# Three of sixteen output-projection blocks in other product forms, and four weight splits on GpSimd

## The chip, the cores and the metric

The kernel runs on one core of one Trainium2 chip. The metric is the device time of one execution in microseconds (us), as the median of the runs shown. TensorE (PE) multiplies, and its weight loads (PEld) are recorded apart from its matmuls. VectorE (DVE), ScalarE (ACT) and GpSimd (POOL) work elementwise, and SyncE (SP) issues most of the DMA transfers.

## What is computed

One layer of a streaming encoder runs for 256 frames of a new stream and 64 frames of a running one, 320 positions in all; all matrices are 32-bit floats. What the change touches is the output projection behind the merge of two branches, and its residual add:

```
def layer(x, l, cache_k, cache_v, norm_mix, w_in, b_gate, ..., w_out, norm_ffn, w_gate_up, w_down):
    ...
    merged = g_a * (a @ w_branch_a[l]) + g_b * (bb @ w_branch_b[l])
    h = x + merged @ w_out[l]
    hn = rmsnorm(h, norm_ffn[l])
    gu = hn @ w_gate_up[l]
    ...
```

`merged` is 320 x 2048 and `w_out` is 2048 x 2048.

## The kernel before, in words

Features lie on partitions and the 320 positions (`T`) in the free dimension. A weight matrix is cut into blocks of 128 output features; the host lays each block out as 128 x (chunks x 128). `block` (L87) multiplies one block with all its chunks of 128 input features and sums the products in one PSUM tile `acc` of which three exist. The blocks follow one another in the order of the program: the input projection, its two branches, `w_out`, then the feed-forward weights. The output projection is the loop `for m in range(KD)` at L659 to L666, sixteen blocks of sixteen chunks.

A 32-bit product is made of three matmuls in the rounded 32-bit type `F32R`. Every activation is kept as a high and a low part, and every weight tile is split in the same way while it streams in. `weights` (L68) fetches eight chunks (a half-block, 128 x 1024, 512 KB) on SP's queue into `raw`, of which there are three buffers. ACT casts it to `wh` (L75) and DVE subtracts to get `wl` (L76); there are four buffers of each. `product` (L80) then issues, for one chunk, `wh` times the high part (L83), `wh` times the low part (L84) and `wl` times the high part (L85), each 320 columns wide. In the output projection the high and low parts are named `mh` and `ml`. So a half-block has 24 matmuls and a block 48.

Some small matmuls elsewhere take plain 32-bit operands (`F32`) and are not split: the diagonal attention scores (L416), part of the attention output (L488), the gating mix (L602, L604), and the sums at the end (L721, L723). The trace prints the type of both kinds as f32, so the line tells which it is; a plain 32-bit matmul of the program stands in the trace as two matmul records, each with its own weight load (L604 is called 16 times and has 32 records).

After each block of the output projection, DVE adds the residual `xr` (L664), ACT and DVE split the result times a gain for the feed-forward part (`gained`, L121), ACT squares it (L197) and GpSimd adds the square to a running sum (L198). The residual's tile `xr` is fetched on the same SP queue as the weights (L662).

A scheduler of the tile framework sets the order on each engine and the waits between them, from the order in which the code is written and the number of buffers of each tile. Instructions marked `keep_in_program_order` stay in the order of the code.

Of the kernel before, what the change touches and what calls it, by code (L numbers as in the profile page):

```python
# [8 lines left out]
F32 = mybir.dt.float32  # L9
# [4 lines left out]
P = 128  # L14
TP = 256
TS = 64
T = TP + TS
D = 2048
KD = D // P
H = 8  # L20
HALF = 8
# [12 lines left out]
def stream_step(ctx: ExitStack, tc: tile.TileContext, xT, w_in, w_a, w_b, w_out, w_gu, w_down,  # L34
                gains, ws_t, bs, ck_t, cv, y_t, k_t, v_t, sv_t):
    nc = tc.nc
    pool = lambda name, bufs=1, **kw: ctx.enter_context(tc.tile_pool(name=name, bufs=bufs, **kw))
    const = pool("const")
    wraw = pool("wraw", 3)
# [5 lines left out]
    def acc():  # L45
        return psum.tile([P, 512], F32, tag="acc", bufs=3, name="acc")

    def aux():
        return psum.tile([P, 512], F32, tag="aux", bufs=4, name="aux")

    def aux1():
        return psum.tile([P, 512], F32, tag="aux1", bufs=1, name="aux1")
# [9 lines left out]
    def tick():  # L62
        state["tick"] += 1
        for fn, a in later.pop(state["tick"], ()):
            fn(*a)


    def weights(src, n, view=lambda t: t):  # L68
        raw = wraw.tile([P, HALF * P], F32, tag="raw", name="raw")
        d = nc.sync.dma_start(out=view(raw[:, : n * P]), in_=src)  # L70
        if state["tick"] < 4:
            tc.keep_in_program_order(d)
        wh = wsplit.tile([P, HALF * P], F32R, tag="wh", name="wh")
        wl = wsplit.tile([P, HALF * P], F32R, tag="wl", name="wl")
        nc.scalar.copy(out=wh[:, : n * P], in_=raw[:, : n * P])  # L75
        nc.vector.tensor_tensor(out=wl[:, : n * P], in0=raw[:, : n * P],  # L76
                                in1=wh[:, : n * P].bitcast(F32), op=ALU.subtract)
        return wh, wl

    def product(ps, w, j, x, first, last):  # L80
        wh, wl = w
        a, b = wh[:, j * P : (j + 1) * P], wl[:, j * P : (j + 1) * P]
        nc.tensor.matmul(ps[:, :T], a, x[0], start=first, stop=False)  # L83
        nc.tensor.matmul(ps[:, :T], a, x[1], start=False, stop=False)  # L84
        nc.tensor.matmul(ps[:, :T], b, x[0], start=False, stop=last)  # L85

    def block(src, act):  # L87

        ps = acc()
        nk = len(act)  # L90
        for k0 in range(0, nk, HALF):
            n = min(HALF, nk - k0)
            w = weights(src[:, k0 * P : (k0 + n) * P], n)
            for j in range(n):
                product(ps, w, j, act[k0 + j], k0 + j == 0, k0 + j == nk - 1)
            tick()
        return ps[:, :T]
# [23 lines left out]
    def gained(tag, src, gain):  # L121
        hi, lo = slot(tag), slot(tag)
        nc.scalar.activation(out=hi, in_=src, func=AF.Copy, scale=gain)  # L123
        nc.vector.scalar_tensor_tensor(out=lo, in0=src, scalar=gain, in1=hi.bitcast(F32),
                                       op0=ALU.mult, op1=ALU.subtract)
        return hi, lo

    def t320(tag, bufs=2, dt=F32):
        return tmp.tile([P, T], dt, tag=tag, bufs=bufs, name=tag)
# [431 lines left out]
    for g in range(H):  # L561
        ps = block(w_in[4 * H + g], xs)
# [61 lines left out]
    for g in range(H):  # L624
        ps = block(w_in[3 * H + g], xs)
# [6 lines left out]
    merged = []  # L632
    for m in range(KD):
        gate = []
        for i in range(2):
            ps = block(w_in[5 * H + i * KD + m], xs)
# [8 lines left out]
        ps = block(w_a[m], [aT[h] for h in range(H)])  # L645
        t = t320("mg", 1)
        nc.vector.tensor_tensor(out=t, in0=ps, in1=gate[0], op=ALU.mult)
        ps = block(w_b[m], [bT[g] for g in range(H)])
# [11 lines left out]
    for m in range(KD):  # L660
        x = t320("xr")
        tc.keep_in_program_order(nc.sync.dma_start(out=x, in_=xT[:, m, :]))  # L662
        ps = block(w_out[m], merged)
        nc.vector.tensor_tensor(out=hs[m], in0=ps, in1=x, op=ALU.add)  # L664
        hg.append(gained("A", hs[m], g_ffn[:, m : m + 1]))
        sq.add(hs[m], nc.vector if m == KD - 1 else None)  # L666
# [10 lines left out]
    for s0, n in SLICES:  # L677
        act = []
# [17 lines left out]
        for m in range(KD):  # L696
            ps = block(w_down[m][:, s0 * P : (s0 + n) * P], act)
# [20 lines left out]
    ps, cols = aux1(), aux()  # L718
    keep(nc.tensor.matmul(cols[:, 1:2], mones, tiny, start=True, stop=False, skip_group_check=True))
    for i, t in enumerate((sqf.total, last)):  # L720
        keep(nc.tensor.matmul(ps[:, inner], mones, t[:, inner], start=i == 0, stop=i == 1))  # L721
        for c, r in enumerate(COLS):
            keep(nc.tensor.matmul(cols[0 : r.stop - r.start, c : c + 1], t[:, r], mones[:, 0:1], start=False,  # L723
                                  stop=i == 1, skip_group_check=True))
# [15 lines left out]
    for c, r in enumerate(COLS):  # L740
        keep(nc.tensor.matmul(far[:, r], col[:, c : c + 1].to_broadcast([P, P]), ident[:, 0 : r.stop - r.start],
                              start=c == 0, stop=c == 1, skip_group_check=True))
# [83 lines left out]
```

## Time and profile before

| what | value |
|---|---|
| median of 2 runs | 1701.62 us (1701.53 to 1701.71) |
| span of the profiled execution | 1700.0 us |
| PE busy | 1690.0 us, 11550 matmul records |
| DVE busy | 881.0 us |
| ACT busy | 673.2 us |
| POOL busy | 58.4 us |
| output projection (16 blocks), from its first matmul to the next stage's | about 645.8 to 758.4 us |
| bytes read from HBM | 256.03 MB |

The profiled execution's span is 1.6 us under the median of the timed runs, which holds what lies around the span as well. Durations of matmul records are pipelined: one lasts longer than the distance to the next, so what a matmul costs on PE is read from starts or from the chain of waits, not from its duration.

### The profile page before, as it was taken

Reading aid. Unit: us, or ns where it says so; the run is one execution under the profiler, and the core shown is the slowest. Engines: PE = TensorE matmul, PEld = TensorE weight load, DVE = VectorE, ACT = ScalarE, POOL = GpSimd, SP = SyncE. Lnnn points to the kernel's source line nnn. Section 1 sums busy time; section 2 is a strip of 40 time slices with the busy share of each in tenths; the row PEclk is TensorE's granted clock in tenths of the full one; section 3 lists DMA queues with packets and bytes.
Section 4 is the critical chain, followed back from the end, with each engine's and each line's share of the span. In section 5 each row is a group of like instructions: output and inputs, shape, how many; then the busy total and the mean of one; then the engine's idle time right before and its main releaser. Section 6 shows DMA issues by size and latency. Waiting matters only on the chain.

```text
span 1700.0 us, 27477 instructions
## 1 busy us (share of the span) xinstructions
PE 1690.0 (99%) x11550; PEld 1689.2 (99%) x11550; DVE 881.0 (52%) x1150; ACT 673.2 (40%) x885; POOL 58.4 (3%) x81
## 2 busy tenths in 40 slices
PE   9999999999999999999999999999999999999997
PEld 9999999999999999999999999999999999999997
DVE  6677656544444445555444444444444444444455
ACT  6655545433333333443333332333333323333342
POOL 0300021000000000110000000000000000000000
PEclk9999999999999999999999999999999999999999
DMA  6676556544444455554444455444444554444453
GB/s 249 195 219 173 172 168 173 147 151 152 150 150 151 150 156 165 173 164 149 150 149 150 150 152 150 151 151 149 150 149 149 149 149 150 150 152 149 132 150 124
DMA packets 100507, 268.30 MB, mean 158 GB/s; under 512 B 28992, under 2 KB 35392, under 8 KB 100384
## 3 DMA queue, kind: packets, MB, share of 16 engines
q1 hardware_dynamic: 97936, 261.36, 49.8%
q0 software_dynamic: 1312, 3.80, 0.7%
q8 instruction: 90, 1.47, 0.4%
q10 hardware_dynamic: 1136, 1.39, 0.2%
q14 instruction: 33, 0.27, 0.0%
HBM read 256.03 MB, written 5.51 MB: 154 GB/s over the span
## 4 chain that ended last, share of the span: by engine, by line
PE 99%; DVE 0%; DMA 0%; ACT 0%; DVEq 0%; issue 0%
PE acc L84 32%; PE acc L83 32%; PE acc L85 32%; PE aux L243 2%; PE acc L243 1%; PE aux L488 1%; DVE h L749 0%; PE aux L604 0%; DMA gain<-gains 0%; PE aux L418 0%; PE aux L421 0%; PE aux L416 0%; PE aux L602 0%; PE aux L721 0%; ACT A L123 0%; ACT wh L233 0%
## 5 line engine op out<-in xcount | busy, mean ns | idle before, releaser
L75 ACT CAST wh<-raw 128x1024 fp32r<-128x1024 f32 x468 | 484.4, 1036 | 922.8 <-PE acc L84 746.6
L76 DVE TENSOR_TENSOR wl<-raw,wh 128x1024 fp32r<-128x1024 f32 x468 | 564.8, 1207 | 476.0 <-ACT wh L75 475.3
L83 PE MATMUL acc<-A,wh 128*128 128x320 f32 x2464 | 762.0, 309 | 0.0
L85 PE MATMUL acc<-A,wl 128*128 128x320 f32 x2464 | 761.4, 309 | 0.0
L84 PE MATMUL acc<-A,wh 128*128 128x320 f32 x2464 | 761.4, 309 | 0.0
L83 PEld LDWEIGHTS acc<-A,wh 128*128 128x128 f32 x2464 | 462.5, 188 | 0.0
L84 PEld LDWEIGHTS acc<-A,wh 128*128 128x128 f32 x2464 | 462.5, 188 | 0.0
L85 PEld LDWEIGHTS acc<-A,wl 128*128 128x128 f32 x2464 | 462.5, 188 | 0.0
L83 PE MATMUL acc<-B,wh 128*128 128x320 f32 x960 | 296.6, 309 | 0.0
L84 PE MATMUL acc<-B,wh 128*128 128x320 f32 x960 | 296.6, 309 | 0.0
L85 PE MATMUL acc<-B,wl 128*128 128x320 f32 x960 | 296.6, 309 | 0.0
L83 PEld LDWEIGHTS acc<-B,wh 128*128 128x128 f32 x960 | 180.2, 188 | 0.0
L84 PEld LDWEIGHTS acc<-B,wh 128*128 128x128 f32 x960 | 180.2, 188 | 0.0
L85 PEld LDWEIGHTS acc<-B,wl 128*128 128x128 f32 x960 | 180.2, 188 | 0.0
L83 PE MATMUL acc<-mh,wh 128*128 128x320 f32 x256 | 79.1, 309 | 0.0
L84 PE MATMUL acc<-ml,wh 128*128 128x320 f32 x256 | 79.1, 309 | 0.0
L85 PE MATMUL acc<-mh,wl 128*128 128x320 f32 x256 | 79.1, 309 | 0.0
L683 DVE TENSOR_TENSOR ev<-acc,rh 128x320 f32<-128x320 f32 x44 | 21.6, 492 | 56.6 <-PE acc L85 56.6
L686 DVE TENSOR_TENSOR bb<-acc,rh 128x320 f32<-128x320 f32 x44 | 21.6, 492 | 56.5 <-PE acc L85 56.5
L83 PEld LDWEIGHTS acc<-mh,wh 128*128 128x128 f32 x256 | 48.0, 188 | 0.0
L84 PEld LDWEIGHTS acc<-ml,wh 128*128 128x128 f32 x256 | 48.0, 188 | 0.0
L85 PEld LDWEIGHTS acc<-mh,wl 128*128 128x128 f32 x256 | 48.0, 188 | 0.0
(184 smaller groups left out, 732.5 us busy)
## 6 DMA issues: line engine op xcount, KB each, us to landing
raw<-w_gu SPq DMA_DIRECT2D x176, 512.0 KB, 3.6
raw<-w_in SPq DMA_DIRECT2D x141, 512.0 KB, 3.7
raw<-w_down SPq DMA_DIRECT2D x80, 512.0 KB, 3.6
raw<-w_out SPq DMA_DIRECT2D x32, 512.0 KB, 3.6
raw<-w_a SPq DMA_DIRECT2D x16, 512.0 KB, 3.6
raw<-w_b SPq DMA_DIRECT2D x16, 512.0 KB, 3.5
raw<-w_down SPq DMA_DIRECT2D x16, 256.0 KB, 2.6
x<-xT SPq DMA_DIRECT2D x8, 320.0 KB, 7.6
```

The costliest lines, as they stand in the source:

```text
L75: nc.scalar.copy(out=wh[:, : n * P], in_=raw[:, : n * P])
L76: nc.vector.tensor_tensor(out=wl[:, : n * P], in0=raw[:, : n * P], in1=wh[:, : n * P].bitcast(F32), op=ALU.subtract)
L83: nc.tensor.matmul(ps[:, :T], a, x[0], start=first, stop=False)
L84: nc.tensor.matmul(ps[:, :T], a, x[1], start=False, stop=False)
L85: nc.tensor.matmul(ps[:, :T], b, x[0], start=False, stop=last)
L243: nc.tensor.matmul(first[b][h][:, :T], w[:, (h * n + j) * P : (h * n + j + 1) * P], xs[c + j][i], start=not last and c + j + i == 0, stop= ...
L488: mm = lambda out, a, b, first, last: nc.tensor.matmul(out, a, b, start=first, stop=last, skip_group_check=True)
L683: nc.vector.tensor_tensor(out=t, in0=pg, in1=got["rh"], op=ALU.mult)
L686: nc.vector.tensor_tensor(out=u, in0=pu, in1=got["rh"], op=ALU.mult)
```

## The change

Line numbers of the changed kernel are those of the old one plus 2 in `product`, plus 32 behind the new functions and plus 35 behind the changed loop. In the output projection, block 4 goes through `exact` over one piece of 320 columns, block 8 through `exact` over two pieces of 160 columns, and block 12 through `halved` over two pieces of 160. `exact` takes the unsplit weight tile `raw` as a plain 32-bit operand and multiplies it with the high and the low part of the activation, also as plain 32-bit operands. `halved` keeps the three products of the split form but issues each as two matmuls of 160 columns. In blocks 2 and 3 the subtraction that makes `wl` goes to GpSimd; the other thirteen blocks' splits and products stay as they were, except that blocks 4 and 8 need no split.

```
+    pooled = [False]
+
...
-        nc.vector.tensor_tensor(out=wl[:, : n * P], in0=raw[:, : n * P],
+        (nc.gpsimd if pooled[0] else nc.vector).tensor_tensor(out=wl[:, : n * P], in0=raw[:, : n * P],
                                 in1=wh[:, : n * P].bitcast(F32), op=ALU.subtract)
...
+    def exact(src, act, widths):
+
+        ps = acc()
+        for k0 in range(0, KD, HALF):
+            raw = wraw.tile([P, HALF * P], F32, tag="raw", name="raw")
+            nc.sync.dma_start(out=raw, in_=src[:, k0 * P : (k0 + HALF) * P])
+            for j in range(HALF):
+                w = raw[:, j * P : (j + 1) * P]
+                for i in range(2):
+                    for c in widths:
+                        nc.tensor.matmul(ps[:, c], w, act[k0 + j][i][:, c].bitcast(F32),
+                                         start=k0 + j + i + c.start == 0, stop=k0 + j + i == KD,
+                                         skip_group_check=True)
+            tick()
+        return ps[:, :T]
+
+    def halved(src, act, widths):
+
+        ps = acc()
+        for k0 in range(0, KD, HALF):
+            wh, wl = weights(src[:, k0 * P : (k0 + HALF) * P], HALF)
+            for j in range(HALF):
+                for w, i in ((wh, 0), (wh, 1), (wl, 0)):
+                    for c in widths:
+                        nc.tensor.matmul(ps[:, c], w[:, j * P : (j + 1) * P], act[k0 + j][i][:, c],
+                                         start=k0 + j + i + c.start == 0 and w is wh,
+                                         stop=k0 + j == KD - 1 and w is wl, skip_group_check=True)
+            tick()
+        return ps[:, :T]
...
-        ps = block(w_out[m], merged)
+        whole, parts2 = (slice(0, T),), (slice(0, T // 2), slice(T // 2, T))
+        form = {4: (exact, whole), 8: (exact, parts2), 12: (halved, parts2)}.get(m)
+        pooled[0] = m in (2, 3)
+        ps = form[0](w_out[m], merged, form[1]) if form else block(w_out[m], merged)
```

How the instructions move is shown at three places. The first is PE at the start of block 8, in the changed program; a row of a plain 32-bit matmul here is one instruction of the program, which the trace records twice.

```order
L86 MATMUL acc<-ml,wh 128x320
L87 MATMUL acc<-mh,wl 128x320
L99 MATMUL acc<-mh,raw 128x160 x2
L99 MATMUL acc<-ml,raw 128x160 x2
L99 MATMUL acc<-mh,raw 128x160 x2
```

The block before ends in the old triple; then each chunk has four 32-bit matmuls of 160 columns on the unsplit tile, where the old program had three of 320. Block 4 has the same with one row of 128x320 for each part.

The second is PE at the start of block 12.

```order
L86 MATMUL acc<-ml,wh 128x320
L87 MATMUL acc<-mh,wl 128x320
L113 MATMUL acc<-mh,wh 128x160 x2
L113 MATMUL acc<-ml,wh 128x160 x2
L113 MATMUL acc<-mh,wl 128x160 x2
```

The order of the three products stays, and each stands twice, over half the columns.

The third is GpSimd in the changed program, from the gating part to the first norm of the feed-forward part.

```order
L616 DMA sv_t<-vown 128x64 x8
L78 TENSOR_TENSOR wl<-raw,wh 128x1024 x4
L230 TENSOR_TENSOR sq_h<-sq_h,sq 128x320 x14
L201 TENSOR_TENSOR root<-ms,mhalf 32x10
L768 TENSOR_TENSOR power<-mean,mhalf 128x2
```

The four subtractions of blocks 2 and 3 stand ahead of all fourteen square additions of the output projection; before the change the square additions followed the `sv_t` stores directly.

## The prediction

> **What bounds the kernel now.** I read the page first (busy shares, clock, chain that ended last), then the stretch in which the change lies, then the chain piece by piece.
>
> ```profile
> span 1700.0 us, 27477 instructions
> ...
> PE 1690.0 (99%) x11550; PEld 1689.2 (99%) x11550; DVE 881.0 (52%) x1150; ACT 673.2 (40%) x885; POOL 58.4 (3%) x81
> ...
> PEclk9999999999999999999999999999999999999999
> ...
> PE 99%; DVE 0%; DMA 0%; ACT 0%; DVEq 0%; issue 0%
> ```
>
> PE is the path: 99% of the chain, at the full granted clock in every slice. The stretch of the output projection says the same, PE without a gap, DVE busy for 56% of it and ACT for 41%.
>
> ```profile
> core 0: us, PE busy (x) PEld busy (x) DVE busy (x) ACT busy (x) POOL busy (x), PEclk, DMA share, GB/s
> 645.78:758.35 112.57, 112.57 (x769) 112.57 (x769) 63.54 (x65) 46.44 (x63) 15.21 (x14) 1.00 0.54 170
> ```
>
> So time changes only by what PE itself takes, unless a feeder falls behind. A matmul's duration overlaps the next one's, so its price comes from the chain of waits, which cuts PE's time into pieces that add up: start, length, line and count.
>
> ```profile
> 16.39 3.55 PE acc L243 x24
> ...
> 191.66 0.22 PE aux L416 x2
> 191.88 0.36 PE aux L418 x3
> ...
> 192.83 0.58 PE aux L421 x4
> ```
>
> L243, L418 and L421 are split-form (F32R) matmuls: over 320 columns 0.58/4 = 0.145 us, and 3.55/24 = 0.148 with the start's small waits; 112.57/(16 x 48) = 0.1466 for the projection itself. I use 146.6 ns, so a block is 48 x 0.1466 = 7.04 us. Over 256 columns the price is 0.36/3 = 0.120. L416 is one plain 32-bit (F32) matmul over 128 columns: two records, 0.11 us each.
>
> **The change part by part.** Three blocks, 3 x 7.04 = 21.1 us, are replaced.
>
> *What a weight load sets as a floor.* Every matmul record has its own load, also where the tile is the same as just before: L83 and L84 both multiply `wh`.
>
> ```profile
> L83 PEld LDWEIGHTS acc<-mh,wh 128*128 128x128 f32 x256 | 48.0, 188 | 0.0
> L84 PEld LDWEIGHTS acc<-ml,wh 128*128 128x128 f32 x256 | 48.0, 188 | 0.0
> ```
>
> How fast loads can follow each other is seen where the matmuls are short. The timeline has a run of eight records over 64 columns (F32):
>
> ```profile
> 245.03 1.00 PE L488 MATMUL aux<-wt,cv 128*128 128x64 f32 x8
> 245.03 0.86 PEld L488 LDWEIGHTS aux<-wt,cv 128*128 128x128 f32 x7
> ...
> 192.54 0.60 PEld L421 LDWEIGHTS aux<-B 128*128 128x128 f32 x4
> ```
>
> Seven loads take 0.86 us and one lasts 0.192, so they start (0.86 - 0.192)/6 = 0.111 us apart. That is also the price of 128 columns (0.11), so 64 and 128 columns cost the same: the load is the floor, 111 ns. At 320 columns (L421) the loads are paced by the matmuls instead.
>
> *What a plain 32-bit record streams per column.* No F32 matmul of the trace is wider than 128, and at 128 the floor hides the streaming. The durations by form are the nearest evidence: min, median, max in ns.
>
> ```profile
> L723 PE MATMUL aux<-mones,sq_f x4: 169/207/250, 1688.1 to 1688.4; 128*128 128x1 f32 x2, 128*64 128x1 f32 x2
> ...
> L488 PE MATMUL aux<-wt,cv x32: 222/275/275, 115.0 to 245.8; 128*128 128x64 f32 x32
> ...
> L604 PE MATMUL aux<-wst,vsn x32: 275/275/275, 279.0 to 314.8; 128*128 128x128 f32 x32
> ...
> L418 PE MATMUL aux<-B x24: 281/285/365, 62.2 to 192.5; 128*128 128x256 f32 x24
> ...
> L421 PE MATMUL aux<-B x16: 305/308/309, 63.2 to 193.1; 128*128 128x320 f32 x16
> ```
>
> The unhindered minima of F32 grow from 169 (1 column) over 222 (64) to 275 (128): 0.84 and 0.83 ns per column. F32R grows from 281 (256) to 309 (320): 0.44. So a 32-bit record streams a column in about twice the time, and a 32-bit product has two such records. Ends are modelled, so this is a lean, not a proof.
>
> *Block 4* (F32, 320 columns): 16 chunks x 2 parts x 2 records = 64 records. Streaming is 320 x 0.83 = 266 ns; F32R's price stands 146.6 - 320 x 0.44 = 6 ns over its streaming, which gives 272; twice the F32R price gives 293. I take 275, near the first: 64 x 0.275 = 17.6 us, so +10.6. Bounds: 146.6 (no dearer than F32R) gives 9.4, +2.3; 293 gives 18.8, +11.7.
>
> *Block 8* (F32, 2 x 160): 128 records. Streaming 133 ns, over the floor of 111, so the load hides; with the same 6 ns 139, and half of 293 is 146.6. I take 141: 18.05 us, +11.0. Bounds: the floor, 111, gives 14.2, +7.2; 146.6 gives +11.7.
>
> The Trainium skill, FP8 and Floating Point Precision, section TensorE Precision Notes, says that true 32-bit products take four passes through the array. Read as four F32R passes a product over 320 columns would be 4 x 146.6 = 586 ns against my 550, and both blocks +11.7, the upper bounds above, 1.8 us more in the sum.
>
> *Block 12* (F32R, 2 x 160): 96 records. A column at 0.44 ns makes 70 ns of streaming, under the load's floor: 111 each, 10.7 us, +3.6. That is the nearest row, a narrow matmul with a 128 x 128 32-bit load. Bounds: 73 (half of 146.6, loads hidden) gives 7.0, +0; the price of a whole F32 product over 160, 282 ns, gives 27.1, +20.0, since no F32R matmul of the trace is narrower than 256.
>
> The Trainium skill, TensorE: Matmul & The Clock Gate, section Back-to-back issue gap, gives a sustained 81 ns for a load and matmul over 128 columns, which speaks against my floor. By it block 12 would take 96 x 0.081 = 7.8 us and cost +0.7; the L488 run at 111 ns disagrees.
>
> *Splits on GpSimd and what feeds PE.* Rows of groups, the longest waits, and the transfers of the weights:
>
> ```profile
> L390 POOL TENSOR_TENSOR B<-k,B 128x320 fp32r<-128x320 f32 x7 | 7.6, 1089 | 13.7 <-ACT B L389 13.6
> ...
> L749 POOL TENSOR_TENSOR h<-h,near 128x256 f32<-128x256 f32 x3 | 2.1, 716 | 0.0
> L76 DVE TENSOR_TENSOR wl<-raw,wh 128x1024 fp32r<-128x1024 f32 x32 | 39.2, 1226 | 27.5 <-ACT wh L75 27.5
> L75 ACT CAST wh<-raw 128x1024 fp32r<-128x1024 f32 x32 | 33.6, 1051 | 66.1 <-PE acc L84 62.8 <-issue 3.3
> ACT wh L75 <- PE acc L84: 746.6, 343, 2.5
> raw<-w_out SPq DMA_DIRECT2D x32, 512.0 KB, 3.6
> ...
> L198 POOL TENSOR_TENSOR sq_v<-sq_v,sq x7: 875/979/1550, 212.3 to 246.9; 128x320 f32<-128x320 f32 x7
> ```
>
> GpSimd does the same subtraction over 320 columns in 1.089 us, so over 1024 in 3.48 (by L749's 256 columns 2.86) against DVE's 1.23. The cast waits for PE: it starts when PE has left the buffer used four half-blocks before, so three half-blocks, 3 x 3.52 = 10.6 us, lie between that and PE's need. Cast and subtraction take 1.05 + 3.48 = 4.5, and one subtraction fits a half-block's 3.52. I cost the edit at nothing: PE's earlier half-blocks cover it. Without that cover it would cost 3.48 - 1.23 = 2.25 us each, 9 us. Behind the four stand the square additions, and the square tile has one buffer, so ACT's next square waits for them: the last subtraction ends about 4.7 us after block 1, the addition some 1.1 later, and block 2's square comes after 7.
>
> Blocks 4 and 8 hold two of three `raw` buffers until PE has used them; the next halves pass through the third, one at a time: 3.6 + 1.05 + 1.23 = 5.9 us each. They have block 4's 17.6 us for it, instead of two half-blocks of 3.52. On SP, the residual `xr` fetches stand behind those transfers; the only waiter is DVE's residual add, and three `acc` buffers leave PE two blocks ahead. Cost: nothing; the 2 x (1.05 + 1.23) us of split work saved per block is off the path and gains nothing either.
>
> *Sum.* 10.6 + 11.0 + 3.6 = +25.2 us: the span goes from 1700.0 to 1725.2, and the median, which stands 1.6 higher, from 1701.6 to 1726.8.
>
> **Rivals.**
> - *Narrow F32R loses its rate.* Below some width between 160 and 256 each record of block 12 costs as much as a 32-bit product, 282 ns: +20.0 instead of +3.6, 1701.6 + 10.6 + 11.0 + 20.0 = 1743.2, slower by 2.4%. It decides against "no change" from 1735.6, a record price of (7.04 + 12.4)/96 = 203 ns. For it: no row is narrower than 256 in that type. Against it: 256 and 320 columns lie on one line with the streaming (0.120 and 0.1466), with no step in sight.
> - *A 32-bit record streams like F32R*, and only its load binds: 2.3 + 7.2 + 3.6 = +13.1, 1714.7. For it: 64 and 128 columns are priced alike. Against it: the durations' growth.
> - *Repeated loads are dropped* where the second half uses the tile of the first: with the cheap streaming too, block 12 costs +0, block 8 128 x 0.073 = 9.4 (+2.3) and block 4 +2.3, 1706.2, no change to speak of. Against it: L83 and L84 load the same tile twice.
> - *GpSimd falls behind.* The four subtractions end 1.05 + 4P after the first cast starts, and the last is wanted 10.6 + 3 x 3.52 + 0.3 = 21.5 after it, so it decides from P = 5.1 us. At twice the estimate, 7.0, PE waits 7.5 us: 1734.3. For it: the additions `sq_v` on the same engine range from 0.875 to 1.550 us for one size. Against it: 1.6 us of room per subtraction.
>
> **How the numbers follow.** Forecast 0.66; narrow F32R 0.20; cheap 32-bit streaming 0.06; dropped loads 0.02; GpSimd late 0.03; something else 0.03. The forecast's own range is 1724 to 1730: block 4 by 266 or 293 ns a record, block 8 by 137 or 146.6, block 12 by 108 to 118. For 8 in 10 the range must reach the narrow-F32R case with its own spread, so 1722 to 1745; the two cheap cases, 0.08, are left out. Two per cent, about what a measurement of this kernel can tell from no change, is 34 us, so slower begins at 1735.6: slower 0.22 (narrow F32R and a part of the rest), same 0.77, faster 0.01, as nothing on PE gets shorter.
>
> **What would show it.** In the groups of the changed kernel, the 32-bit line has 64 records over 320 and 128 over 160 columns, and the halved line 96. In the chain, a record costs near 0.275, 0.141 and 0.111 us; the stretch of the sixteen blocks takes 112.6 + 25.2 = 137.8 us with PE without a gap. A price of 0.147 over 320 in block 4 is the cheap rival, 0.28 in block 12 the narrow one. Idle time of PE that GpSimd ends in blocks 2 or 3, or a subtraction above 5 us, is the fourth. A gap after blocks 4 or 8 released by ACT, DVE or a `raw` transfer would prove my account of the buffers wrong.

## The result and the profile after

The changed kernel takes 1726.28 us (median of 2 runs, 1726.07 to 1726.48) against 1701.62: a ratio of 1.0144, 95% interval 1.0115 to 1.0174. The forecast was 1726.8 in a range of 1722 to 1745, and the side was "within 2%", which holds.

The page of the changed kernel, the same rows as those of before (busy times with counts of records, clock, engines of the chain):

```profile
span 1724.7 us, 27758 instructions
...
PE 1715.0 (99%) x11694; PEld 1708.8 (99%) x11694; DVE 870.2 (50%) x1142; ACT 669.4 (39%) x881; POOL 66.9 (4%) x85
...
PEclk9999999999999999999999999999999999999999
...
PE 99%; DMA 0%; DVE 0%; SPq 0%; ACT 0%; issue 0%; DVEq 0%
```

PE has 144 records more, as counted (64 + 128 + 96 for 144), and is still the whole path. The stretch of the output projection, by engine, from its first matmul to the next stage's, before and after (the prediction's window of it, 112.57 us, was 0.07 narrower at its edges):

```profile
645.76:758.40 112.64, 112.64 (x770) 112.64 (x769) 63.54 (x65) 46.44 (x63) 15.21 (x14) 1.00 0.54 170
```

```profile
core 0: us, PE busy (x) PEld busy (x) DVE busy (x) ACT busy (x) POOL busy (x), PEclk, DMA share, GB/s
646.30:783.13 136.83, 136.83 (x914) 131.76 (x913) 53.32 (x57) 42.78 (x59) 23.57 (x18) 1.00 0.43 140
```

It lasts 136.83 us instead of 112.64, +24.2, with PE busy in all of it. PEld is no longer without gaps: over 320 columns of plain 32-bit a load lasts 190 ns and a record takes 269, so the loads wait. The chain of waits gives each new block as one piece (start, length, line, records):

```profile
674.62 17.23 PE acc L99 x64
712.96 17.39 PE acc L99 x128
751.46 10.69 PE acc L113 x96
```

That is 269 ns a record for plain 32-bit over 320 columns, 135.9 over 160, and 111.4 for split-form over 160. Together 45.3 us in place of 21.1: +24.2, the whole of the stretch's growth. The span grew by 24.7. The other half microsecond came before: the stretch begins at 646.30 here and at 645.76 in the profile of before, and in the seven kernels below, which differ from these only in the output projection, its start lies anywhere from 645.4 to 646.4. It is scatter of the start of the program: a hundred matmul records in, PE stands at 17.97 us here and at 17.44 before, and from there to the stretch the two take the same time.

### The profile page after: what moved, and what is told of

Its sections match the earlier page's. It is cut to its first block, busy times and chain, and to the rows that moved or that the text cites. A ratio compares the mean times of both kernels' runs of the same rounds, so it can differ in the third digit from the quotient of the medians.

```text
span 1724.7 us, 27758 instructions
## 1 busy us (share of the span) xinstructions
PE 1715.0 (99%) x11694; PEld 1708.8 (99%) x11694; DVE 870.2 (50%) x1142; ACT 669.4 (39%) x881; POOL 66.9 (4%) x85
## 4 chain that ended last, share of the span: by engine, by line
PE 99%; DMA 0%; DVE 0%; SPq 0%; ACT 0%; issue 0%; DVEq 0%
PE acc L86 31%; PE acc L85 31%; PE acc L87 31%; PE acc L99 2%; PE aux L275 2%; PE acc L275 1%; PE acc L113 1%; PE aux L520 1%; DMA raw<-w_in 0%; DVE h L784 0%; PE aux L636 0%; PE aux L450 0%; PE aux L453 0%; PE aux L448 0%; SPq L254 0%; PE aux L634 0%
## 5 line engine op out<-in xcount | busy, mean ns | idle before, releaser
L78 DVE TENSOR_TENSOR wl<-raw,wh 128x1024 fp32r<-128x1024 f32 x460 | 554.8, 1206 | 498.3 <-ACT wh L77 496.1
L85 PE MATMUL acc<-mh,wh 128*128 128x320 f32 x208 | 64.6, 311 | 0.0
L86 PE MATMUL acc<-ml,wh 128*128 128x320 f32 x208 | 64.3, 309 | 0.0
L87 PE MATMUL acc<-mh,wl 128*128 128x320 f32 x208 | 64.3, 309 | 0.0
L739 DVE TENSOR_TENSOR h<-acc,h 128x320 f32<-128x320 f32 x47 | 23.0, 489 | 46.5 <-PE acc L87 46.5
L85 PEld LDWEIGHTS acc<-mh,wh 128*128 128x128 f32 x208 | 39.0, 188 | 0.1
L86 PEld LDWEIGHTS acc<-ml,wh 128*128 128x128 f32 x208 | 39.0, 188 | 0.1
```

Source lines behind the costliest of these rows:

```text
L78: (nc.gpsimd if pooled[0] else nc.vector).tensor_tensor(out=wl[:, : n * P], in0=raw[:, : n * P], in1=wh[:, : n * P].bitcast(F32), op=ALU.s ...
L739: nc.vector.tensor_tensor(out=hs[m], in0=ps, in1=hs[m], op=ALU.add)
```

## The experiments

The theory to be tested: a record's price is the larger of a floor set by its weight load and a streaming time set by its columns and its type; everything else in the change is covered. The rivals were those of the prediction. In every kernel of this section the loop's selection line is what is edited, and unless said otherwise DVE makes all splits.

**Is any of it GpSimd's?** The first kernel keeps the four GpSimd subtractions and drops the new forms; the second gives all sixteen blocks' subtractions to GpSimd.

```
-        form = {4: (exact, whole), 8: (exact, parts2), 12: (halved, parts2)}.get(m)
+        form = None                      # both kernels
         pooled[0] = m in (2, 3)          # first kernel
+        pooled[0] = True                 # second kernel, False again behind the loop
```

> Only the four subtractions of blocks 2 and 3 go to GpSimd; all sixteen blocks keep the three split products over 320 columns. Theory (PE's records alone make the 24.7 us, the splits lie under PE's earlier half-blocks): 1701.6 us within 0.5, PE without a gap in the output projection, a GpSimd subtraction of 2.4 us as in the changed kernel. Rival (part of the 24.7 us is GpSimd's): 1702.5 to 1711, with PE waiting for a subtraction in blocks 2 or 3.

> All sixteen blocks of the output projection are split on GpSimd, all in the old product form. Theory: GpSimd needs 2 x 2.40 for the subtractions and 1.09 for the square addition, 5.9 us of a block's 7.04, so it keeps up: 1701.6 within 1 us. Rival (it falls behind when it also has the additions in every block, or its subtraction lengthens to 3 us and more when it runs without pause): each block loses up to 1 us, 1705 to 1718.

The first took 1701.63 us against 1701.56 for the kernel before, ratio 0.9999 (0.999 to 1.0009); the second 1702.79 in a single run. Their stretches of the output projection and their GpSimd subtractions (min, median, max in ns), the first kernel's two fences and then the second's:

```profile
645.94:758.58 112.64, 112.64 (x770) 112.64 (x769) 61.75 (x61) 46.43 (x63) 24.89 (x18) 1.00 0.55 170
```

```profile
L78 POOL TENSOR_TENSOR wl<-raw,wh x4: 2398/2405/2409, 650.7 to 661.2; 128x1024 fp32r<-128x1024 f32 x4
```

```profile
646.37:759.01 112.64, 112.64 (x771) 112.64 (x769) 47.95 (x36) 46.45 (x63) 85.08 (x44) 1.00 0.55 171
```

```profile
L78 POOL TENSOR_TENSOR wl<-raw,wh x32: 2398/2406/2407, 637.0 to 746.1; 128x1024 fp32r<-128x1024 f32 x32
```

Both stretches last 112.64 us, to the hundredth that of before, with 32 subtractions as with four, though GpSimd is then busy for 85.08 us of it. So the splits cost nothing, and the second kernel's higher time does not come from them: its stretch begins later (646.37), its span is 1700.6, and its time stands 2.2 us over its span, where the profiled execution of the first kernel stands 1.7 over its own. That single time lies 0.2 us outside the 1 us that was allowed; the rival asked for 1705 and PE gaps, of which there are none.

**Do the prices hold when every block has the form?** Two kernels, all sixteen blocks plain 32-bit over 320 columns, and all sixteen in halves of 160.

```
-        form = {4: (exact, whole), 8: (exact, parts2), 12: (halved, parts2)}.get(m)
+        form = (exact, whole)            # third kernel
+        form = (halved, parts2)          # fourth kernel
```

> All sixteen blocks use plain 32-bit products over 320 columns on unsplit weights; no split on GpSimd. Theory (64 records of 269 ns a block, buffers no matter): a block takes 17.2 us instead of 7.04, 16 x 10.2 = +163, 1864.5 us, within 2. Rival (the weight tiles held until PE has used them starve PE once blocks of this form follow each other, or the split weights behind the last one come late): some us of gaps on top, 1868 and more. Rival (records get cheaper in a long run, as the two parts share a load): under 1855.

> All sixteen blocks use the three split products, each over 2 x 160 columns; no split on GpSimd. Theory (96 records at the weight load's floor of 111.4 ns): 10.7 us a block instead of 7.04, 16 x 3.66 = +58.6, 1760.2 us, within 1.5. Rival (a record's price depends on what runs beside it, and one block was lucky): off by more than 3 us either way.

They took 1865.46 and 1760.69 us. The chains:

```profile
645.89 275.63 PE acc L99 x1024
```

```profile
646.00 171.49 PE acc L113 x1536
```

1024 records in one piece make 269.2 ns each, 1536 make 111.6. The stretches grew by 163.0 and 58.9 us, where 163 and 58.6 were expected. The totals lie 1.0 and 0.5 above. In the third kernel the start is no later than before (645.73); 0.8 us stands at the very end, where 4.7 us pass between DVE's last addition and the end of the span instead of 3.9, behind all matmuls. In the fourth, 0.3 lies in the stretch, and the rest is not placed. In the third kernel DVE and ACT have almost nothing to do in the stretch (21 and 18 of 276 us), and every weight tile is held until PE is through with it. A record still costs what it did in one block alone, and no gap opens. The buffers cost nothing here, and no load is saved by the two parts that follow each other on one tile.

**Does narrow split-form lose its rate?** Three blocks over uneven pieces.

```
+        cut = lambda n: (slice(0, n), slice(n, T))
-        form = {4: (exact, whole), 8: (exact, parts2), 12: (halved, parts2)}.get(m)
+        form = {4: (halved, cut(192)), 8: (halved, cut(240)), 12: (halved, cut(256))}.get(m)
```

> Three blocks use the split products over two uneven pieces: block 4 over 192 and 128 columns, block 8 over 240 and 80, block 12 over 256 and 64; no split on GpSimd. Theory (a record costs the larger of the load's floor of 111 ns and 0.458 ns a column, which cross near 243 columns): 111 ns for 64, 80, 128, 192 and 240, and 118 for 256; blocks of 10.7, 10.7 and 11.0 us, +3.6, +3.6 and +4.0, 1712.8 us. Rival (the rate changes with the width, below 256 columns): 192 and 240 dearer than 111, in the worst case near 160 and 200 ns (two clocks a column), +2.4 and +4.3 on top, 1719 or more. Rival (a narrow record streams in its own time when it follows a wide one, the load hidden under the wide one): block 8 and 12 near 48 x (111 + 37) = 7.1 us, 1705.5.

It took 1712.71 us. The chain's three blocks, 192 + 128, 240 + 80 and 256 + 64 columns:

```profile
673.87 10.67 PE acc L113 x96
705.70 10.65 PE acc L113 x96
737.54 10.81 PE acc L113 x96
```

A pair costs 222, 222 and 225 ns. Two floors are 222 to 223, so the pairs cost what two floors make, down to 64 columns and up to 240; with 256 the wide one begins to show. The trace prices only the pair: starts within one are uneven (about 142 and 81 ns in turn in the first block), so 111 for each of the two is the theory's reading of the sum. The narrow-rate rival wanted 2.4 us more in the first block and 4.3 in the second; the hidden-load rival wanted 7.1 us. Neither is there.

**Is the floor the load, and what does a column cost?** Extra matmuls in old-form blocks, 16 in each half-block, weights and moving columns both from the split weight tiles, into a PSUM tile without a reader. This is added work; what the kernel computes stays.

```
...
+            for j in range(HALF):
+                for h in w:
+                    nc.tensor.matmul(more[0:rows, :n], h[:, j * P : j * P + rows], w[0][:, :n],
+                                     start=True, stop=True)
...
```

Here `n` is the moving columns and `rows` the weight columns. In the second probe both operands are also reread as the type that is priced, `F32R` or `F32`.

> Six blocks of the old form have 32 matmuls more each, on split weights as both operands, into a PSUM tile that nothing reads (extra work, the outputs are the reference's): over 512, 384 and 320 columns with 128 weight columns, and over 320, 160 and 64 columns with 64 weight columns. Theory (a load's floor goes with the weight columns, and split-form records stream at 0.458 ns a column): 235, 176, 147, 147, 73 and 55 ns, 32 x 0.733 = +23.5 us, 1725. Rival on the rate (a record streams a column per clock, 0.417, and each load costs some 13 ns on top): 227, 173 and 147 over 512, 384 and 320, and near 140 over 320 with the half load. Rival on the floor (it is a price per record, not the load): 111 over 160 and over 64 with 64 weight columns.

> The 32 extra matmuls of the first probe in eight blocks (extra work, the outputs are the reference's), to map what a split-form record costs above a column per clock: over 288 and 448 columns with 128 weight columns, over 256, 224, 192 and 128 with 64, and as plain 32-bit matmuls over 512 columns with 128 weight columns and 96 with 64. Theory (0.458 ns a column up to some 320 columns, beyond that a column per clock with some 14 ns on top): 132, 201, 117, 103, 88 and 59 ns. Rival (a column per clock and some 13 ns on every record): 133, 200, 120, 107, 93 and 67. For the plain 32-bit ones (two records each, two clocks a column and 2.4 ns): 429 and 82 ns a record. Together 32 x 0.700 + 64 x 0.511 = +55.1 us, 1756.8.

They took 1728.19 and 1757.32 us. The six prices of the first text sum to 833 ns, not the 733 it wrote, so its theory meant 1728.3. Pieces of the chain, each the 16 records of one half-block: over 512, 384 and 320 columns with 128 weight columns, then over 320, 160 and 64 columns with 64.

```profile
663.37 3.65 PE acc L128 x16
...
684.74 2.78 PE acc L128 x16
...
704.39 2.35 PE acc L128 x16
...
723.16 2.34 PE acc L128 x16
...
741.94 1.18 PE acc L128 x16
...
758.42 0.90 PE acc L128 x16
```

The second probe: split-form over 288 and 448 columns with 128 weight columns, over 256, 224, 192 and 128 with 64, then plain 32-bit over 512 with 128 and over 96 with 64 (32 records each).

```profile
663.15 2.11 PE acc L128 x16
...
681.44 3.24 PE acc L128 x16
...
694.95 1.83 PE acc L128 x16
...
705.65 1.65 PE acc L128 x16
...
723.05 1.42 PE acc L128 x16
...
740.01 0.96 PE acc L128 x16
...
756.09 13.73 PE acc L128 x32
...
797.62 2.78 PE acc L128 x32
```

The floor goes with the weight columns: over 160 columns a record costs 111 with 128 of them (block 12 above) and 74 with 64, and over 64 columns 56 with 64 (inside the piece starts are 58 apart), about half of 111. That the probe's records differ in other ways is no objection: over 320 columns with 128 weight columns they cost the 147 of the kernel's own. A price of 111 per record whatever it loads is refuted.

For the streaming, the table sets the price per split-form record against N / 2.4 ns, where N is the columns. That is a column per clock if the full clock is 2.4 GHz, as the Trainium skill states in TensorE: Matmul & The Clock Gate, section Wait — 56ns, not 53.3ns?. The plain 32-bit prices fit that figure at two clocks a column: 135.9, 269.2 and 429 ns over 160, 320 and 512 columns lie on a line of 0.833 ns a column, with some 2.5 ns left over.

| columns (weight columns) | price, ns | above N / 2.4 |
|---|---|---|
| 128 (64) | 60 | 7 |
| 160 (64) | 74 | 7 |
| 192 (64) | 89 | 9 |
| 224 (64) | 103 | 10 |
| 256 (64) | 114 | 8 |
| 288 (128) | 132 | 12 |
| 320 (128) | 147 | 14 |
| 320 (64) | 146 | 13 |
| 384 (128) | 174 | 14 |
| 448 (128) | 202 | 16 |
| 512 (128) | 228 | 15 |

My 0.458 ns a column fails above 320 (235 expected at 512, 228 measured), so it is not one rate for all widths; a column per clock with something on top comes nearer. The rival's fixed 13 ns fails at 256 and below (7 to 10), and its lighter half load fails too: 146 and 147 over 320. The surplus grows, not evenly, from 7 to 14 ns up to some 320 columns and then stays near 15; what makes it stays open. All rows up to 256 columns have the half load; a full and a half load were compared over the same columns at 320 alone, and at 256 by the pair above, which leaves 114 for the wide record. The plain 32-bit records cost 429 over 512 columns (two clocks a column are 427). Over 96 the piece, its edges included, makes 87; starts inside it are 82 to 83 apart (two clocks a column are 80).

## Why the prediction was right

- **PE is the path and the change's records are the cost.** Shown: the three pieces of the chain hold all 24.2 us of the stretch, and the GpSimd half of the change alone moved nothing.
- **The load's floor, 111 ns.** Predicted 10.7 us for block 12, measured 10.69. That it is the load is shown by the half loads, that it holds for narrow split-form by the sixteen-block kernel and, as the sum of a pair, by the uneven widths.
- **Two clocks a column for a plain 32-bit record.** Right; it had rested only on modelled durations, 0.83 ns a column. Measured are 269 ns over 320 columns, 135.9 over 160 and 429 over 512, that is 0.84 to 0.85, or 0.833 from one width to the next. That the modelled durations came so near is in part luck: the 275 ns over 128 columns were no unhindered minimum, as L488's records over 64 columns last 275 too where the load paces them (111 ns from one to the next), and L416, over 128, has a minimum of 270, which would have made 0.75.
- **Blocks 4 and 8, the mis-sized terms.** 17.6 and 18.05 us were predicted, 17.23 and 17.39 measured, 1.0 us too much together. The step that failed is the surcharge: I took 6 ns from the split form, whose surplus is its own, and rounded up to 275 and 141. A plain 32-bit record carries 2 to 3 ns over two clocks a column.
- **Four passes and 81 ns.** Two records make 538 ns for a plain 32-bit product over 320 columns. The four passes of the Trainium skill, FP8 and Floating Point Precision, section TensorE Precision Notes, at split-form price, an estimate, would have been 586. Four passes fit if one costs 134.5 ns, less than a split-form record. With a full load a record costs 111 over 160 columns, and a pair over 192 and 128 costs 222; with half a load one over 128 columns costs 60. The sustained 81 ns over 128 columns of the Trainium skill, TensorE: Matmul & The Clock Gate, section Back-to-back issue gap, does not hold for these 32-bit loads.
- **GpSimd, costed at nothing.** Right, by a wider margin than argued: a subtraction took 2.40 us, not 3.48; the time did not grow in proportion from 320 columns (1.09) to 1024.
- **The buffers, costed at nothing.** Right: ACT did wait for weights while blocks 4 and 8 held their tiles, and PE did not. The changed kernel's groups of the stretch show both, the cast with what ended its idle time and the long matmuls without any:

```profile
L77 ACT CAST wh<-raw 128x1024 fp32r<-128x1024 f32 x28 | 29.4, 1049 | 75.1 <-PE acc L86 36.3 <-DMA raw<-w_out 29.5 <-PE acc L113 7.7
L99 PE MATMUL acc<-ml,raw 128*128 128x160 f32 (+1 forms) x96 | 22.5, 344 | 0.0
```

  29.5 us of ACT's idle time ended with a weight transfer, where the same row of before named none. They lie before eight casts, from 667.7 to 723.0 us, that is just ahead of and in blocks 4 and 8.
- **The sum.** +25.2 predicted. Measured +24.2 in the stretch and half a microsecond of scatter at the start: blocks 4 and 8 were 1.0 too dear in the sum, and a late start hid half of that. The closeness of 1726.8 to 1726.28 is partly luck, worth about 0.5 us.
- **The rivals.** Narrow split-form at 282 ns: 111.4. A 32-bit record as cheap as a split-form one: 269 against 147. Dropped repeated loads: 111 a record in block 12, where halves share a tile. GpSimd late: no gap with all 32 subtractions.

## What to carry to other kernels

Where PE is the path, price a matmul record as the larger of its weight load (111 ns here for 128 columns of 32 bits, about half for 64) and its streaming, and count records: cutting the moving side below the crossing, here between 240 and 256 columns for a split-form record, buys nothing per record and doubles the loads. A plain 32-bit product (blocks 4 and 8 have two to a chunk) cost two records of two clocks a column, 538 ns over 320 columns, against 440 for three split-form records, so the split pays at this width as long as other engines have room to make the halves. When no row shows a price at the size in question, take the slope over sizes from the same type, and do not carry a surcharge over from another.

## What the runs showed that was not expected

The split-form record is 13 to 14 ns dearer over 320 columns than a column per clock at 2.4 GHz, with a full or a half weight load. Over the 11550 records of the kernel before, nearly all of this form and width, that is by estimate some 150 us, 9% of the time; plain 32-bit records carry only 2 to 3 ns over two clocks a column. No run here tells where it comes from.
